# A hybrid attention trunk on one core: the last stage merges in wide chunks through scratch memory, then projects tile by tile

## The chip, the cores and the metric

The kernel runs on 1 core of one Trainium2 chip. The metric is device time in microseconds of one execution. The kernel before was timed in 3 runs: median 3657.09 us, 3652.93 to 3662.06.

## The reference, cut to what matters

One layer of an encoder for two groups of tokens: a prompt of 16 meta tokens and 2048 tokens, and 8 sample streams of 16 tokens. The kernel keeps them as 17 tiles of 128 tokens (0 to 15 of the prompt, and `s`).

```
(g_q, g_k, g_v, g_low, g_r, d_q, d_k, d_v, i_q, i_k, i_w, d_z, m_a, m_b) = split(h @ w_in)
o_a = gla_recurrence(...)                      # branch A, gated linear attention
y_a = (rmsnorm(o_a) * silu(g_r)) @ w_gla
o_b = attend(...)                              # branch B, attention over the 256 best keys
y_b = (o_b * silu(d_z)) @ w_dsa
merged = sigmoid(m_a + gate_b[0]) * y_a + sigmoid(m_b + gate_b[1]) * y_b
h_new  = layer_norm(ALPHA * h + merged @ w_out, ln_g, ln_b)
```

The last three products, with `w_gla`, `w_dsa` and `w_out` (1024 x 1024 each), are the stage that is changed. Every operand of a product is split into a high part (`h`, rounded to the format that TensorE takes) and the rest (`l`); a product is three matmuls, high by high, high by low and low by high.

## The kernel before, in words

Phase 1 makes the projections of `w_in` and writes them to scratch tensors in device memory (names `d_...`). Phase 2 runs the attention of branch B by blocks of 128 queries, from block 15 down to 8, with the recurrence of branch A beside it. The change begins where that ends (about 2690 us): the blocks of `LAST` (7, 6, 5, 0, 4, 2, 1, 3) are attended, and between them the generator `gla_project` is advanced, by the number that stands beside each block.

`gla_project` (L1355) makes `y_a`, gated: for each chunk of tokens (`PASSA` of them) it loads and splits the chunk's `d_oa` into the four pairs `xh`, `xl` (`x3`, L1333), and for each of 8 slices of 128 output channels it runs a group of 24 matmuls into the PSUM tile `pd` (`proj3`, L1349), multiplies by the row of gates `rma` (from `d_ma`) on VectorE and writes the result to `d_ya`. The slice's weights, 128 x 128, stand still in TensorE; the chunk's tokens are the moving columns, so a chunk's width is the matmul's width.

`finish` (L1385) then does the last stage in chunks of 256 tokens (one of 128). `merge` (L1373) is one chunk: 8 groups of 24 matmuls with `w_dsa`, and behind each group a multiply by `rmb` and an add of `rya` (VectorE), a rounding to `mgh` (ScalarE) and the rest `mgl` (GpSimd); `mgh` and `mgl` stay in SBUF, in two sets (`pm0`, `pm1`). The projection of a chunk takes, for each tile of 128 tokens, 48 matmuls of 512 columns into `fo` (L1413), and then the layer norm on VectorE and the store. Merges run two chunks ahead of it, so TensorE always has both kinds of matmul to choose from. `w3` (L1316) loads a weight matrix in 16 pieces, each through a raw buffer, a cast on ScalarE and a subtraction on VectorE or GpSimd.

The order on each engine is not the order of the code: a scheduler lays all instructions out by the code's order as priority and by when it reckons each is ready. Every engine then runs its list in order. All DMAs of this part are issued by one engine, SP, in order too; a load into a buffer waits there until the buffer is free, and what stands behind it waits along. Tile pools on the left and on the right of SBUF are stacks: a pool that is opened where another was closed waits for the last use of what lay there.

Of the kernel before, what the change touches and what calls it, by code (L numbers as in the profile page):

```python
# [10 lines left out]
F32 = mybir.dt.float32  # L11
F32R = mybir.dt.float32r
# [5 lines left out]
OP = mybir.AluOpType  # L18
PSUM = bass.MemoryType.PSUM
DRAM = bass.MemoryType.DRAM  # L20

P = 128
DM = 1024
KT = 8
META = 16
# [11 lines left out]
ALPHA = 2.0 ** 0.25  # L37
# [5 lines left out]
TURNS = "DAA", "DDA"  # L43
KLOW = 1040
HALF = 8
LAST = [(7, 0), (6, 2), (5, 1), (0, 1), (4, 2), (2, 1), (1, 1), (3, 0)]
NP3 = 256
EARLY = 1500
SKB = 3
POOL = "pkqx"  # L50
# [1 line left out]
PDB = 1  # L52
# [6 lines left out]
FKB = 3  # L59
WOM = 512  # L60
WOD = 1
KLAG = 1
FPACE = -5
PASSA = 9
SHORT = 8
NEARLY = 13
IDX_SCALE = (8 ** -0.5) * (64 ** -0.5)
TOPK = 256
# [6 lines left out]
ORDER = [t for p in PIECES for t in p if t != "m"]  # L75
NT = len(ORDER)
TT = META + NT * P
COL = {t: META + i * P for i, t in enumerate(ORDER)}
# [7 lines left out]
def nkeys(j):  # L86
    return META + P * (j + 1)
# [31 lines left out]
class Trunk:  # L119
# [73 lines left out]
    def scratch(self, ctx):  # L193
        dr = ctx.enter_context(self.tc.tile_pool(name="dr", bufs=1, space=DRAM))
        d = {}
        for n, s, t in (
            ("gq", [512, TT], F32), ("gk", [512, TT], F32), ("gl", [16, TT], F32), ("lf", [512, TT], F32),
            ("gv", [TT, 1024], F32), ("gr", [TT, 1024], F32),
            ("q", [2048, TT], F32R),
            ("ih", [512, TT], F32R), ("il", [512, TT], F32R),  # L200
            ("kd", [P, 4, TT], F32R), ("v", [TT, 256], F32), ("z", [TT, 1024], F32),
            ("ma", [1024, TT], F32), ("mb", [1024, TT], F32),
            ("oa", [1024, TT], F32), ("ob", [1024, TT], F32), ("ya", [1024, TT], F32), ("h", [TT, 1024], F32),
        ):
            d[n] = dr.tile(s, t, name="d_" + n)
        d["mask"] = {j: dr.tile([P, nkeys(j)], BF16, name=f"d_mask{j}") for j in range(16)}
        d["mask"]["s"] = dr.tile([P, SKEY], BF16, name="d_masks")
        d["xt"] = [dr.tile([P, KT, n], F32, name=f"d_xt{q}") for q, n in enumerate(PCN)]
        self.d = d
# [1027 lines left out]
    def phase2(self):  # L1237
        nc, tc, d = self.nc, self.tc, self.d
        with ExitStack() as main:
            early = ExitStack()  # L1240
            left = lambda n, bufs=1, **kw: early.enter_context(tc.tile_pool(name=n, bufs=bufs, **kw))
# [7 lines left out]
            right = lambda n, bufs=1, **kw: main.enter_context(tc.tile_pool(name=n, bufs=bufs, side="right", **kw))  # L1249
# [44 lines left out]
            inner.close()  # L1294
            tail = ExitStack()
            left = lambda n, bufs=1, **kw: tail.enter_context(tc.tile_pool(name=n, bufs=bufs, **kw))
            self.pm, self.pd = [left("pm0")], left("pd", PDB, space=PSUM)
            if PDB == 1:
                self.px.append(left("px2", space=PSUM))
            self.pw2, self.px3, self.pr, self.pe, self.pw = left("pw2"), left("px3"), left("pr", PRB), left("pe", 2), left("pw")  # L1300
            self.pm.append(left("pm1"))
            steps, self.turns = self.gla_project(), TURNS[1]
            next(steps)
            for j, n in LAST:
                for _ in self.attend(j):
                    pass
                for _ in range(n):
                    next(steps, None)
            self.flush()
            fin = self.finish()  # L1310
            next(fin)
        next(fin, None)
        tail.close()


    def w3(self, pool, src, name, width, most=512, raws=None, last=None):  # L1316
# [16 lines left out]
    def x3(self, name, c0, n):  # L1333

        xh = [self.px3.tile([P, 2, NP3], F32R, name=f"xh{k}") for k in range(4)]
        xl = [self.px3.tile([P, 2, NP3], F32R, name=f"xl{k}") for k in range(4)]
        for k in range(4):
            raw = self.pr.tile([P, 2, NP3], F32, name="raw")
            self.nc.sync.dma_start(raw[:, :, :n], self.d[name][2 * k * P : (2 * k + 2) * P, c0 : c0 + n].rearrange("(k p) t -> p k t", p=P))
# [3 lines left out]
    def rows3(self, name, c0, n, q):  # L1343

        t = self.pe.tile([P, NP3], F32, name="r" + name, tag="rb" if name == "mb" else "ra")
        self.nc.sync.dma_start(t[:, :n], self.d[name][q * P : (q + 1) * P, c0 : c0 + n])
# [8 lines left out]
    def gla_project(self):  # L1355

        ws = self.w3(self.pw, self.i["w_gla"][0], "w", P, last=self.pw2)
        w = -(-(TT - META) // (2 * PASSA)) * 2

# [10 lines left out]
                self.nc.sync.dma_start(self.d["ya"][q * P : (q + 1) * P, c0 : c0 + n], g)  # L1370
            yield

    def merge(self, wd, x, c0, n, pool):  # L1373

        mh = pool.tile([P, KT, NP3], F32R, name="mgh")
        ml = pool.tile([P, KT, NP3], F32R, name="mgl")
        for q in range(8):
            ya = self.rows3("ya", c0, n, q)
            t = self.rows3("mb", c0, n, q)
            self.tt(t, self.proj3(wd[q], x, n), t, OP.mult)  # L1380
            self.tt(t, t, ya, OP.add)
            self.split_sb(mh[:, q, :n], ml[:, q, :n], t)
        return mh, ml

    def finish(self):  # L1385

        nc, tc, i, d = self.nc, self.tc, self.i, self.d
        chunks = [(COL[j], 2 * P) for j in (15, 13, 11, 9, 7, 5, 1, 3)]
        chunks.insert(SHORT, (COL[0], P))
        x = self.x3("ob", *chunks[0])  # L1390
        wd = list(self.w3(self.pw, i["w_dsa"][0], "w", P, last=self.pw2))
        ready = [self.merge(wd, x, *chunks[0], self.pm[0])]
        ready.append(self.merge(wd, self.x3("ob", *chunks[1]), *chunks[1], self.pm[1]))
        yield
        with ExitStack() as c:
            pool = lambda n, bufs=1, **kw: c.enter_context(tc.tile_pool(name=n, bufs=bufs, **kw))
            cp, wk, pp = pool("fc"), pool("fk", FKB), pool("fo", 4, space=PSUM)
            self.pd = pool("pd2", 2, space=PSUM)
            wo = None
            for q, (c0, n) in enumerate(chunks):  # L1400
                if wo is None:
                    wo = list(self.w3(cp, i["w_out"][0], "wo", 512, WOM, wk))
                    lg = self.bcast_load(cp, i["ln_g"][0], DM, "lg3")
                    lb = self.bcast_load(cp, i["ln_b"][0], DM, "lb3")
                mh, ml = ready.pop(0)
                for s in range(0, n, P):
                    t = ORDER[(c0 + s - META) // P]
                    h = wk.tile([P, DM], F32, name="h3")
                    nc.sync.dma_start(h[:], d["h"][c0 + s : c0 + s + P, :])
                    for u in range(2):  # L1410
                        ps = pp.tile([P, 512], F32, name="fo")
                        wh, wl = wo[u]
                        self.mm3(ps[:], lambda k: mh[:, k, s : s + P], lambda k: ml[:, k, s : s + P],  # L1413
                                 lambda k: wh[:, k, :], lambda k: wl[:, k, :], KT)
                        cs = slice(512 * u, 512 * u + 512)
                        self.stt(h[:, cs], h[:, cs], ALPHA, ps[:], OP.mult, OP.add)
                    mu, rstd = self.ln_stats(wk, h[:], DM, P)
                    out = self.o["y_sample"].rearrange("b t d -> (b t) d") if t == "s" else self.o["y_prompt"][0, t * P : (t + 1) * P, :]
                    self.stt(h[:], h[:], mu, lg[:], OP.subtract, OP.mult)
                    cut = 2 if q == len(chunks) - 1 and s + P == n else 1  # L1420
                    for u in range(cut):
                        cs = slice(DM // cut * u, DM // cut * (u + 1))
                        self.stt(h[:, cs], h[:, cs], rstd, lb[:, cs], OP.mult, OP.add)
                        nc.sync.dma_start(out[:, cs], h[:, cs])
                if q + 2 < len(chunks):
                    nx = chunks[q + 2]
                    ready.append(self.merge(wd, self.x3("ob", *nx), *nx, self.pm[q % 2]))

    def setup(self, ctx):
        self.scratch(ctx)  # L1430
# [40 lines left out]
```

## Time and profile before

| | |
|---|---|
| median of 3 runs | 3657.09 us |
| profiled execution | 3653.39 us, its span 3651.6 us |
| busy in the span | PE 3516.6 us (96%), DVE 2568.0 (70%), ACT 1451.5 (40%), POOL 1048.6 (29%) |
| chain of waits, share of the span | PE 75%, DVE 13%, DMA 5% |
| mean granted clock of TensorE | 0.985 of full speed |

PE is TensorE's matmuls, PEld its weight loads, DVE VectorE, ACT ScalarE, POOL GpSimd, SP the engine that issues DMAs. Matmuls are pipelined: a matmul's time in a row is longer than the distance from its start to the next one's, so the cost of a run of matmuls is read from the starts. The same holds, less so, for DVE.

### The profile page before, as it was taken

How to read it: one execution, taken by the hardware profiler on the slowest of the kernel's cores; microseconds unless marked ns; L12 is line 12 of the kernel's file. 1: busy time of each engine (PE TensorE's matmuls, PEld its weight loads, DVE VectorE, ACT ScalarE, POOL GpSimd, SP SyncE). 2: the span in 40 equal slices, each digit the busy share in tenths (PEclk: the TensorE clock that was granted, in tenths of full speed). 3: DMA queues.
4: the chain of work that ended last, by engine and by line, in shares of the span. 5: the costliest groups of instructions: out<-in, count | busy, mean ns of one | idle time of the engine just before them, and what ended most of it. 6: DMA issues, size and time to landing. Idle time of an engine off the chain costs nothing.

```text
span 3651.6 us, 65899 instructions
## 1 busy us (share of the span) xinstructions
PE 3516.6 (96%) x24196; PEld 3224.6 (88%) x24196; DVE 2568.0 (70%) x5971; ACT 1451.5 (40%) x3084; POOL 1048.6 (29%) x1220
## 2 busy tenths in 40 slices
PE   7999999999999999999989999999999999989999
PEld 7999999999999999998976778777778888879998
DVE  7748997799999988943246877777765666555444
ACT  4444223433334234325434555555665443431110
POOL 3122343242343344344301433334410000012221
PEclk9999999999999999999999999999999999999999
DMA  8642443263442345363653333233343345564432
GB/s 266 196 127 84 136 124 96 84 180 106 122 127 75 117 136 166 115 173 122 160 170 106 84 92 85 80 92 85 85 116 89 94 106 138 150 193 140 121 114 62
DMA packets 535810, 448.78 MB, mean 123 GB/s; under 512 B 94032, under 2 KB 507856, under 8 KB 535488
## 3 DMA queue, kind: packets, MB, share of 16 engines
q1 hardware_dynamic: 535488, 444.58, 42.4%
q8 instruction: 190, 3.11, 0.4%
q14 instruction: 132, 1.08, 0.1%
HBM read 288.01 MB, written 156.44 MB: 122 GB/s over the span
## 4 chain that ended last, share of the span: by engine, by line
PE 75%; DVE 13%; DMA 5%; ACT 2%; issue 2%; POOL 1%; SPq 1%; POOLq 0%; DVEq 0%; ACTq 0%
PE pp L266 12%; PE pp L264 12%; PE pp L265 12%; PE oo L1070 6%; PE px L1046 4%; PE pd L264 3%; PE pd L266 3%; PE pd L265 3%; PE pl L1110 2%; PE pl L1111 2%; PE fo L264 2%; PE fo L265 2%; PE fo L266 2%; DVE junk L149 1%; DVE sc L152 1%
## 5 line engine op out<-in xcount | busy, mean ns | idle before, releaser
L149 DVE TENSOR_SCALAR_CACHE_REDUCE junk<-sc,cand 128x272 bf16<-128x272 f32 (+6 forms) x512 | 701.7, 1371 | 17.0
L143 POOL TENSOR_TENSOR wlo<-raw,whi 128x512 fp32r<-128x512 f32 x360 | 487.9, 1376 | 768.0 <-ACT whi L158 704.3
L266 PE MATMUL pp<-whi,xl 128*128 128x256 f32 (+3 forms) x1952 | 560.4, 288 | 4.4 <-DVE xl L143 4.4
L264 PE MATMUL pp<-whi,xh 128*128 128x256 f32 (+3 forms) x1952 | 561.7, 288 | 3.1 <-ACT whi L158 2.1
L264 PE MATMUL pp<-xh,whi 128*128 128x384 f32 (+2 forms) x1728 | 563.0, 326 | 1.4 <-ACT whi L158 1.4
L265 PE MATMUL pp<-xl,whi 128*128 128x384 f32 (+2 forms) x1728 | 563.2, 326 | 0.0
L266 PE MATMUL pp<-xh,wlo 128*128 128x384 f32 (+2 forms) x1728 | 562.1, 326 | 0.1
L265 PE MATMUL pp<-wlo,xh 128*128 128x256 f32 (+3 forms) x1952 | 560.9, 288 | 0.0
L266 PEld LDWEIGHTS pp<-whi,xl 128*128 128x128 f32 (+1 forms) x1952 | 370.4, 190 | 14.6 <-DVE xl L143 6.9
L264 PEld LDWEIGHTS pp<-whi,xh 128*128 128x128 f32 (+1 forms) x1952 | 371.4, 190 | 11.2 <-issue 3.0
L265 PEld LDWEIGHTS pp<-wlo,xh 128*128 128x128 f32 (+1 forms) x1952 | 371.4, 190 | 5.4 <-issue 2.3
L1112 DVE CUSTOM_DVE_ANT_0 lgl<-pl,mkl 128x348 f32<-128x348 f32 (+8 forms) x608 | 297.3, 510 | 83.6 <-PE pl L1111 48.0
L1110 PE MATMUL pl<-kd,q 128*128 128x348 f32 (+14 forms) x800 | 308.1, 388 | 32.7 <-DVE mx L1112 23.9
L264 PE MATMUL pd<-xh,wh 128*128 128x242 f32 (+3 forms) x1152 | 327.9, 285 | 8.6 <-ACT wh L1328 3.8
L264 PEld LDWEIGHTS pp<-xh,whi 128*128 128x128 f32 x1728 | 324.4, 188 | 2.7 <-ACT whi L158 2.0
L266 PE MATMUL pd<-xh,wl 128*128 128x242 f32 (+3 forms) x1152 | 324.6, 282 | 0.8 <-POOL wl L143 0.8
L265 PE MATMUL pd<-xl,wh 128*128 128x242 f32 (+3 forms) x1152 | 325.1, 282 | 0.3 <-DVE xl L143 0.3
L266 PEld LDWEIGHTS pp<-xh,wlo 128*128 128x128 f32 x1728 | 324.1, 188 | 1.2 <-POOL wlo L143 0.4
L265 PEld LDWEIGHTS pp<-xl,whi 128*128 128x128 f32 x1728 | 324.4, 188 | 0.7
L158 ACT CAST whi<-raw 128x512 fp32r<-128x512 f32 (+1 forms) x344 | 199.1, 622 | 314.8 <-DMA raw<-in_w_in 201.3
L155 ACT ACTIVATE lgl<-lgl,mx 128x1040 f32<-128x1040 f32 (+7 forms) x256 | 249.8, 976 | 181.5 <-DVE mx L1114 177.6
L1118 POOL COPY pmeta<-lgl 128x48 f32<-128x48 f32 x256 | 58.7, 229 | 771.4 <-ACT lgl L155 765.0
(250 smaller groups left out, 7842.7 us busy)
## 6 DMA issues: line engine op xcount, KB each, us to landing
raw<-in_w_in SPq DMA_DIRECT2D x360, 256.0 KB, 3.2
q<-d_q SPq DMA_DIRECT2D x272, 128.0 KB, 3.0
d_h<-x SPq DMA_DIRECT2D x17, 512.0 KB, 3.4
d_gv<-en SPq DMA_DIRECT2D x68, 128.0 KB, 2.1
d_gr<-en SPq DMA_DIRECT2D x68, 128.0 KB, 1.8
d_z<-en SPq DMA_DIRECT2D x68, 128.0 KB, 1.7
gr<-d_gr SPq DMA_DIRECT2D x17, 512.0 KB, 3.6
v<-d_gv SPq DMA_DIRECT2D x17, 512.0 KB, 3.9
```

The costliest lines, as they stand in the source:

```text
L143: (eng or self.nc.vector).tensor_tensor(out, a, b, op=op)
L149: (eng or self.nc.vector).tensor_scalar(out, a, s1, s2, op0=op0, op1=op1, **kw)
L155: self.nc.scalar.activation(out, a, f, **kw)
L158: (self.nc.vector.tensor_copy if self.spare else self.nc.scalar.copy)(out, src)
L264: mm(ps, ah(k), bh(k), start=k == 0, stop=False)
L265: mm(ps, ah(k), bl(k), start=False, stop=False)
L266: mm(ps, al(k), bh(k), start=False, stop=k == n - 1)
L1046: nc.tensor.transpose(ps[:, 2 * s + u, :], pe[u][a // KLOW][:, a % KLOW : a % KLOW + P], self.ident[:])
L1070: self.nc.tensor.matmul(oo[0][64 * o : 64 * o + 64, k : k + 2, :], self.v[:, s0 + s, d : d + 64], t[:, 2 * s : 2 * s + 2], start=self.fres ...
L1110: nc.tensor.matmul(ps[:, :m], q[:, u, :], kd, start=True, stop=False)
L1111: nc.tensor.matmul(ps[:, :m], q[:, 2 + u, :], kd, start=False, stop=True)
L1112: nc.vector.tensor_tensor_reduce(lg[z1][:, a : a + m], ps[:, :m], mk[z1][:, a : a + m], 1.0, NEG, OP.add, OP.max, mx[:, s : s + 1])
```

## The change

The merges no longer alternate with the projection. `MERGES` lists five chunks: tiles 13, 14, 15 and `s` (512 tokens), 9 to 12 (512), 6 to 8, 0 to 2 and 3 to 5 (384 each). The high and low parts of a merged chunk go to two new scratch tensors, `d_mh` and `d_ml`; the rounding is written over the buffer of `rya`, the rest over that of `rmb`, and both are written from there. The first chunk is emitted ahead of block 1 in `LAST`, inside the attention; the other four come after it, when `w_out` is being loaded. Then 17 tiles are projected: each tile's `mh` and `ml` (512 KB each) are read back, into one set of buffers (`m0`, which is there early) or three more (`m1`, which lie where the merges' pools lay). `gla_project` runs in 5 chunks (436 tokens, one of 432) for 9 (242, one of 240).

```diff
-LAST = [(7, 0), (6, 2), (5, 1), (0, 1), (4, 2), (2, 1), (1, 1), (3, 0)]
-NP3 = 256
+LAST = [(7, 0), (6, 1), (5, 1), (0, 0), (4, 1), (2, 1), (1, 0), (3, 0)]
+NP3 = 512
-PASSA = 9
-SHORT = 8
+PASSA = 5
+MTB = 3
+MERGES = [(13, 4), (9, 4), (6, 3), (0, 3), (3, 3)]
...
             for j, n in LAST:
+                if j == 1:
+                    next(merges)
                 for _ in self.attend(j):
...
+        self.finish(merges, tail)
...
+    def merges(self):
+        x, wd = None, None
+        for t, n in MERGES:
+            c0, n = COL[t], n * P
+            x = self.x3("ob", c0, n)
+            wd = wd or list(self.w3(self.pw, self.i["w_dsa"][0], "w", P, last=self.pw2))
+            for q in range(8):
+                ya = self.rows3("ya", c0, n, q)
+                t = self.rows3("mb", c0, n, q)
+                self.tt(t, self.proj3(wd[q], x, n), t, OP.mult)
+                self.tt(t, t, ya, OP.add)
+                hi, lo = ya.bitcast(F32R), t.bitcast(F32R)
+                self.split_sb(hi, lo, t)
+                for name, z in ("mh", hi), ("ml", lo):
+                    self.move(self.d[name][q * P : (q + 1) * P, c0 : c0 + n], z)
+            yield
...
+            for _ in merges:
+                pass
+            before.close()
+            m1 = c.enter_context(self.tc.tile_pool(name="fm1", bufs=MTB))
+            for q, t in enumerate(tiles):
+                mp = m1 if q % (MTB + 1) else m0
+                m = [mp.tile([P, KT, P], F32R, name="m" + x) for x in "hl"]
+                for z, name in zip(m, ("mh", "ml")):
+                    self.move(z[:], d[name][:, COL[t] : COL[t] + P].rearrange("(k p) t -> p k t", p=P))
```

What stands on the engines is shown at three places (line numbers of the kernel after are up to 4 higher).

TensorE where the last attention block (3) ends and the next stage begins. `oo` are the products with the values, `pl` and `px` transposes and logits, `pd` the groups of 24. Before:

```order
L266 MATMUL pd<-xh_36807,wl_31690 128x240
L1070 MATMUL oo<-pt,v 64x256
L1070 MATMUL oo<-st_37446,v 64x256
L1070 MATMUL oo<-pt,v 64x256
L1070 MATMUL oo<-st_37446,v 64x256
L1070 MATMUL oo<-pt,v 64x256
L1070 MATMUL oo<-st_37439,v 64x256
L1070 MATMUL oo<-pt,v 64x256
L1070 MATMUL oo<-st_37439,v 64x256
L989 MATMUL pl<-ident,pt 128x128 x4
L1082 MATMUL oo<-pm,vm 128x512
L264 MATMUL pd<-xh_37523,wh_37547 128x256
```

The same place now:

```order
L1112 MATMUL pl<-kd_21205,q 128x264
L1113 MATMUL pl<-kd_21205,q 128x264
L1048 MATMUL px<-ident,lgl 128x128 x8
L1080 MATMUL px<-ident,pmeta 96x128 x3
L1048 MATMUL px<-ident,lgl 128x128 x6
L1080 MATMUL px<-ident,pmeta 96x128
L1072 MATMUL oo<-pt,v 64x256
```

Before, groups of `gla_project` stand between the attention's matmuls to the very end of block 3. Now the last such group (of the first merge) stands 150 matmuls ahead of the end, and all between are the attention's.

TensorE where the merges end and the projection goes on, now (before, `pd` and `fo` rows alternate to the end and there is no such place):

```order
L266 MATMUL pd<-xh_37894,wh_35825 128x384
L267 MATMUL pd<-xl_37898,wh_35825 128x384
L268 MATMUL pd<-xh_37894,wl_35826 128x384
L266 MATMUL fo<-woh_36907,mh 128x512
L267 MATMUL fo<-wol_36908,mh 128x512
```

and the DMAs that SP issues there (`mh_38273` and `ml_38274` belong to the tile that TensorE takes next):

```order
L172 DMA d_mh_75<-rya_38125 128x384
L172 DMA d_ml_76<-rmb_38127 128x384
L172 DMA mh_38273<-d_mh_75 128x8x128
L172 DMA ml_38274<-d_ml_76 128x8x128
L172 DMA mh_38341<-d_mh_75 128x8x128
L172 DMA ml_38342<-d_ml_76 128x8x128
L172 DMA d_mh_75<-rya_38160 128x384
L172 DMA mh_38409<-d_mh_75 128x8x128
```

One tile (48 matmuls of `fo`) is spread among the merges before this place, and 768 rows of `fo` follow it without a `pd` between them; the first load of `mh` here waits for the last `pd` matmul.

SP where `w_dsa` begins to load, now (before, these loads stand at the end of block 3; now at the beginning of block 1's attention):

```order
L1340 DMA raw_35747<-d_ob_72 128x2x512
L1033 DMA z_36177<-d_z_68 128x512
L1340 DMA raw_35751<-d_ob_72 128x2x512
L1371 DMA d_ya_73<-rma_35702 128x432
L172 DMA q_36240<-d_q_63 64x4x128
L1328 DMA raw_35757<-in_w_dsa 128x4x128
```

The first piece of `w_dsa` goes through the same two raw buffers as the chunk's `d_ob`, behind its third and fourth piece, and TensorE has 28 attention matmuls between its last `gla_project` matmul and the first one that needs that piece.

## Rows read from the trace of the kernel before

**Rows 1.** The page: PE's busy tenths in 40 slices of the span.

```profile
PE   7999999999999999999989999999999999989999
```

**Rows 2.** Windows: stretch, length, busy us of each engine, PEclk, DMA share, GB/s.

```profile
3231.00:3240.00 9.00, 2.59 (x17) 1.51 (x13) 3.27 (x5) 2.72 (x5) 0.00 (x0) 0.87 0.58 174
3240.00:3250.00 10.00, 7.83 (x41) 6.75 (x40) 3.64 (x7) 3.96 (x8) 2.53 (x3) 0.78 0.89 272
3250.00:3260.00 10.00, 8.57 (x41) 7.90 (x42) 6.89 (x11) 6.13 (x11) 3.19 (x3) 0.66 0.80 251
...
3230.00:3300.00 70.00, 58.22 (x340) 50.73 (x339) 35.34 (x58) 26.80 (x48) 17.94 (x16) 0.90 0.72 223
...
3295.00:3620.00 325.00, 324.20 (x2153) 298.74 (x2152) 149.19 (x271) 40.85 (x93) 68.27 (x78) 1.00 0.38 114
```

**Rows 3.** Timeline of PE: start us, us, matmul; first and last of unbroken runs.

```profile
1846.87 0.34 PE L265 MATMUL pp<-xl,whi 128*128 128x384 f32 x1
...
1848.95 0.33 PE L265 MATMUL pp<-xl,whi 128*128 128x384 f32 x1
...
3219.99 0.27 PE L264 MATMUL pd<-xh,wh 128*128 128x240 f32 x1
...
3222.57 0.27 PE L266 MATMUL pd<-xh,wl 128*128 128x240 f32 x1
...
3262.03 0.28 PE L264 MATMUL pd<-xh,wh 128*128 128x256 f32 x1
...
3263.58 0.28 PE L265 MATMUL pd<-xl,wh 128*128 128x256 f32 x1
...
3589.04 0.27 PE L266 MATMUL pd<-xh,wl 128*128 128x128 f32 x1
...
3593.17 0.28 PE L264 MATMUL pd<-xh,wh 128*128 128x128 f32 x1
...
3641.22 0.39 PE L265 MATMUL fo<-wol,mgh 128*128 128x512 f32 x1
...
3642.80 0.39 PE L266 MATMUL fo<-woh,mgl 128*128 128x512 f32 x1
```

**Rows 4.** Timeline of PE at the old boundary; in brackets idle before, and its releaser.

```profile
3236.73 0.49 PE L1082 MATMUL oo<-pm,vm 96*128 96x512 f32 x1 [4.12 <-DVE pm L143]
3239.52 0.58 PE L264 MATMUL pd<-xh,wh 128*128 128x256 f32 x1 [2.29 <-ACT wh L1328]
```

**Rows 5.** DMA issues from 2690 us: count, KB each, median us to landing.

```profile
h<-d_h SPq DMA_DIRECT2D x17, 512.0 KB, 4.0
rmb<-d_mb SPq DMA_DIRECT2D x64, 128.0 KB, 2.3
...
d_ya<-rma SPq DMA_DIRECT2D x64, 121.0 KB, 2.6
...
raw<-in_w_dsa SPq DMA_DIRECT2D x16, 256.0 KB, 3.5
```

**Rows 6.** Groups by form, 3240 to 3651 us: busy us, mean ns, idle before.

```profile
L143 POOL TENSOR_TENSOR mgl<-rmb,mgh 128x256 fp32r<-128x256 f32 x64 | 51.3, 802 | 152.5 <-ACT mgh L158 152.5
L143 DVE TENSOR_TENSOR rmb<-rmb,rya 128x256 f32<-128x256 f32 x64 | 27.4, 429 | 1.8
L158 ACT CAST mgh<-rmb 128x256 fp32r<-128x256 f32 x64 | 26.0, 406 | 214.7 <-DVE rmb L143 214.6
L143 DVE TENSOR_TENSOR xl<-raw,xh 128x512 fp32r<-128x512 f32 x28 | 20.9, 745 | 30.1 <-ACT xh L158 29.5
L158 ACT CAST xh<-raw 128x512 fp32r<-128x512 f32 x28 | 17.4, 620 | 28.4 <-PE pd L266 13.8 <-DMA raw<-d_ob 11.5 <-PE fo L265 3.0
```

**Rows 7.** Timeline of DVE in block 3's attention.

```profile
3199.49 0.43 DVE L1112 CUSTOM_DVE_ANT_0 lgl<-pl,mkl 128x264 f32<-128x264 f32 x1
...
3199.84 0.43 DVE L1112 CUSTOM_DVE_ANT_0 lgl<-pl,mkl 128x264 f32<-128x264 f32 x1
...
3200.26 1.28 DVE L1056 COPY pt<-px 128x512 f32<-128x512 f32 x2
3201.46 0.68 DVE L143 TENSOR_TENSOR pt<-z,rs 128x512 f32<-128x512 f32 x1
```

More of the change, by code (lines that the diff above doesn't have):

```diff
@@ L203, in scratch @@
             ("oa", [1024, TT], F32), ("ob", [1024, TT], F32), ("ya", [1024, TT], F32), ("h", [TT, 1024], F32),
+            ("mh", [1024, TT], F32R), ("ml", [1024, TT], F32R),
         ):
@@ L1296, in phase2 @@
             left = lambda n, bufs=1, **kw: tail.enter_context(tc.tile_pool(name=n, bufs=bufs, **kw))
-            self.pm, self.pd = [left("pm0")], left("pd", PDB, space=PSUM)
+            self.pd = left("pd", PDB, space=PSUM)
             if PDB == 1:
@@ L1300, in phase2 @@
             self.pw2, self.px3, self.pr, self.pe, self.pw = left("pw2"), left("px3"), left("pr", PRB), left("pe", 2), left("pw")
-            self.pm.append(left("pm1"))
             steps, self.turns = self.gla_project(), TURNS[1]
             next(steps)
+            merges = self.merges()
             for j, n in LAST:
+                if j == 1:
+                    next(merges)
                 for _ in self.attend(j):
@@ L1309, in phase2 @@
             self.flush()
[L1310 to L1313, printed above, removed]
+        self.finish(merges, tail)
     def w3(self, pool, src, name, width, most=512, raws=None, last=None):
@@ L1371, in gla_project @@
             yield
[L1373 to L1394, printed above, removed]
+    def merges(self):
[14 more added lines that the diff above has]
+            yield
@@ L1395, in finish @@
+    def finish(self, merges, before):
+        nc, i, d = self.nc, self.i, self.d
         with ExitStack() as c:
-            pool = lambda n, bufs=1, **kw: c.enter_context(tc.tile_pool(name=n, bufs=bufs, **kw))
-            cp, wk, pp = pool("fc"), pool("fk", FKB), pool("fo", 4, space=PSUM)
+            pool = lambda n, bufs=1, **kw: c.enter_context(self.tc.tile_pool(name=n, bufs=bufs, side="right", **kw))
+            cp, wk, m0, pp = pool("fc"), pool("fk", FKB), pool("fm0"), pool("fo", 4, space=PSUM)
@@ L1398, in finish @@
             self.pd = pool("pd2", 2, space=PSUM)
[L1399 to L1427, printed above, removed]
@@ new lines, in finish @@
+            wo = list(self.w3(cp, i["w_out"][0], "wo", 512, WOM, wk))
+            lg = self.bcast_load(cp, i["ln_g"][0], DM, "lg3")
+            lb = self.bcast_load(cp, i["ln_b"][0], DM, "lb3")
+            for _ in merges:
+                pass
+            before.close()
+            m1 = c.enter_context(self.tc.tile_pool(name="fm1", bufs=MTB))
+            tiles = [ORDER[ORDER.index(t) + k] for t, n in MERGES for k in range(n)]
+            for q, t in enumerate(tiles):
[3 more added lines that the diff above has]
+                    self.move(z[:], d[name][:, COL[t] : COL[t] + P].rearrange("(k p) t -> p k t", p=P))
+                h = wk.tile([P, DM], F32, name="h3")
+                nc.sync.dma_start(h[:], d["h"][COL[t] : COL[t] + P, :])
+                for u in range(2):
+                    ps = pp.tile([P, 512], F32, name="fo")
+                    self.mm3(ps[:], lambda k: m[0][:, k, :], lambda k: m[1][:, k, :],
+                             lambda k: wo[u][0][:, k, :], lambda k: wo[u][1][:, k, :], KT)
+                    cs = slice(512 * u, 512 * u + 512)
+                    self.stt(h[:, cs], h[:, cs], ALPHA, ps[:], OP.mult, OP.add)
+                mu, rstd = self.ln_stats(wk, h[:], DM, P)
+                out = self.o["y_sample"].rearrange("b t d -> (b t) d") if t == "s" else self.o["y_prompt"][0, t * P : (t + 1) * P, :]
+                self.stt(h[:], h[:], mu, lg[:], OP.subtract, OP.mult)
+                cut = 2 if t == tiles[-1] else 1
+                for u in range(cut):
+                    cs = slice(DM // cut * u, DM // cut * (u + 1))
+                    self.stt(h[:, cs], h[:, cs], rstd, lb[:, cs], OP.mult, OP.add)
+                    nc.sync.dma_start(out[:, cs], h[:, cs])
```

## The prediction

> **What bounds the kernel now.** I read the page's slices first, then the windows of the stretch that changes, then TensorE's timeline in it. TensorE is busy in nine tenths or more of nearly every slice [rows 1], and between 3295 and 3620 us it is busy for 324.2 of 325 us at full clock [rows 2]: there time is the number of matmuls times the distance between their starts, and nothing else. The one hole is the boundary between the last attention block and the last stage. From 3230 to 3300 us TensorE is busy for 58.2 of 70 us, so 11.8 us are idle; and in the windows from 3240 and from 3250 us its granted clock is 0.78 and 0.66, a mixture of its two levels (1.2 and 2.4 GHz) that followed idle time of 4.12 and 2.29 us [rows 2, 4]. Against full clock that loses 2.2 and 3.4 us. The boundary costs 11.8 + 5.6 = 17.4 us.
>
> **Wider matmuls: a sure gain.** Distances between starts, from first and last of unbroken runs [rows 3]: 128 columns (3593.17 - 3589.04) / 37 = 0.112 us; 240 columns 2.58 / 23 = 0.112; 256 columns 1.55 / 13 = 0.119; 384 columns 2.08 / 12 = 0.173; 512 columns 1.58 / 7 = 0.226. So there is a floor of 0.112 us below about 240 columns, and above it 256 more columns cost 0.107 us; 432 and 436 columns I put between 384 and 512, at 0.193 and 0.195.
>
> Gated projection: before, 9 chunks x 8 groups x 24 = 1728 matmuls x 0.112 = 193.9 us. Now 768 x 0.195 + 192 x 0.193 = 186.6 us. Gain 7.3 us.
> Merges: before, 1536 x 0.119 + 192 x 0.112 = 204.5 us. Now 384 x 0.226 + 576 x 0.173 = 186.5 us. Gain 18.0 us.
> The projection keeps its 17 x 48 matmuls of 512 columns. Together 25.3 us less for an engine that bounds this part. The distances are measured, so the ends are narrow: 23 to 27.
>
> The Trainium skill ("TensorE: Matmul & The Clock Gate", section "Wait — 56ns, not 53.3ns?") says that matmuls start N / 2.4 GHz + about 2.5 ns apart: 55.6 ns for 128 columns, 215.7 for 512. By that rule the 1536 matmuls that go would bring 1536 x 2.5 ns = 3.8 us and not 25.3, as the columns stay the same. The rows for 128 and 240 columns disagree with it (0.112 us for both); they are what I go by. It is the fourth rival below.
>
> **The boundary moves.** `w_dsa` and the first merge now start inside block 1's attention, so the end of the attention meets ready weights, and the wait for `wh` (2.29 us) and those behind it go. What stays is the attention's own end: 4.12 us until `pm` [rows 4]. And the first group of the second merge writes PSUM that the attention gives back only after the last `ob`, one VectorE instruction (0.6 to 0.7 us, like the last row of [rows 7]) and a handover later: 1.1 us. With 2 us for the clock (half of 4 us, the smaller of the two windows) that is 7.2 us for 17.4: gain 10.2 us, between 8 and 12.
>
> **What it adds: five gaps on TensorE.**
>
> 1. Start of `w_dsa`. Its first piece comes behind the chunk's `d_ob` in two raw buffers. From the moment the last `gla_project` group has used its first pair of `xh`: cast of a 128x1024 pair 1.1 us and subtraction 1.4 (twice 620 and 745 ns less a start-up) [rows 6], then the third piece of `d_ob`, 512 KB, 4.0 us [rows 5], cast and subtraction 2.5, then the piece of `w_dsa` 3.5 us [rows 5], cast 0.6: about 13.2 us. TensorE has 18 matmuls x 0.193 left of its group and some 30 short attention matmuls: 7.3 us. It waits 5.9 us, and 2 us go to the clock: 7.9. Ends 3 and 11: the 2.29 us of [rows 4], where the same load was late; and all of the 4.0 us load added again.
>
> 2. Block 3's attention without cover. Its last 150 matmuls now stand alone: 46 logit matmuls of 264 columns, 70 transposes, 32 value products of 256 columns of which two run side by side. By [rows 3] that is 46 x 0.122 + 70 x 0.112 + 32 x 0.119 = 17.3 us of TensorE. VectorE has 23 logit passes, starting 0.35 us apart, 9 copies 0.60 apart [rows 7], six more of 0.6 to 0.7 for the two halves' ends, two subtractions of 1.4 for the next chunk, a merge's multiply and add 1.3, and 14 short ones: 23 us. Before, all that ran beside `pd` groups. Now the slower engine sets the pace: at least 5.7 us of TensorE idle, and more as each step of the softmax waits for the one before. I take 9; ends 4 (VectorE runs partly ahead) and 18 (TensorE at half clock needs 35 us for its 17).
>
> 3. The merge's two row buffers. A group's buffers now come free only when both parts have been written to memory. Cycle of one buffer at 384 columns: multiply, add, cast at 1.5 times [rows 6] 0.64 + 0.64 + 0.61, GpSimd 1.2 (a scaled-up 802 ns, so an upper value), the write 2.6, the reload 2.3 [rows 5], handovers 0.4: 8.4 us. Two groups of TensorE take 48 x 0.173 = 8.3 us: no reserve, and SP issues four DMAs for each group, in order, each waiting in it; behind it the next group's writes queue. The two PSUM buffers let TensorE run one group ahead, and the 48 matmuls of the first tile (10.8 us) fill in between. While `w_out` loads (16 pieces through three buffers, between the merge's own DMAs on SP and ScalarE) the second merge is as tight. I take 3 us, between 0 and 20.
>
> 4. Changes of chunk inside the merges: four pieces of `d_ob` through two raw buffers again. Two of the changes have the first tile's matmuls beside them, the last has none: 1.5 us, between 0 and 4.
>
> 5. Merges to projection. The first `mh` after the merges goes to where the last weights of `w_dsa` lie, and waits for the last `pd` matmul. Then 0.4 us of issue and 512 KB, 4.0 us [rows 5], with `ml` 0.5 us behind it: 5 us idle, 2 us of clock: 7, between 5 and 9. Behind that load on SP stand the next tiles' loads, which only that tile's successors wait for.
>
> At nothing I count the tiles that follow: a tile is 48 x 0.226 = 10.8 us of TensorE, and its 2 MB of traffic (`mh`, `ml`, `h`, result) makes 190 GB/s, where [rows 2] shows 272 in one window; four sets of buffers give each load 30 us. If that cover goes, each us late in 16 tiles costs 16 us. The end of the kernel (layer norm of the last tile) is as it was.
>
> Sum: -25.3 - 10.2 + 7.9 + 9 + 3 + 1.5 + 7 = -7.1 us. From the profiled execution's 3653.4 us this makes 3646; the median of the runs shown is 3.7 us above that execution, so for a median I say **3650 us**.
>
> **Rivals.**
>
> A. The gaps are smaller than I make them, since the scheduler's list leaves TensorE some attention to do: gap 1 costs 3, gap 2 only the difference of the two engines at 4.5, gap 3 nothing, gap 4 1, gap 5 without clock 5. Sum 13.5 for 28.4, so 22 us less than before: 3635. For it speaks that TensorE was busy through all attention blocks before [rows 1]; against it, that the list puts nothing between the rows of block 3's end.
>
> B. The other side: the write and reload of the merges becomes the bound. With all DMAs on one queue and writes landing like the 512 KB loads do (4.0 us for 2.6), the cycle is 9.8 to 10.1 us for 8.3 of TensorE. That costs 0.8 to 0.9 us for each of 24 groups, about 20 us, less the filling tile where it helps, and some 5 us in the second merge: 16 more than the sum, 3666. It decides from a cycle of about 8.9 us on, where the gain of 7 is used up. For it: the reserve is nil. Against it: the old rows of 128 KB landed in 2.3 us while the stretch moved 114 GB/s [rows 2, 5], and two PSUM buffers.
>
> C. Block 3 falls to the lower clock for all of its bare stretch: gap 2 costs 18, sum +2, 3659: no change that can be measured. For it, the drop to 0.66 and 0.78 after idle time of 2 to 4 us [rows 2, 4].
>
> D. The rule on distances holds and the wide matmuls bring 3.8 us: sum +14.4, 3671. The measured 0.112 us at 128 columns speaks against it.
>
> **How the numbers follow.** 0.3% is about what a measurement of this kernel can tell from no change, 11 us: 3646 to 3668. My forecast (3642 to 3657) has 0.45, A 0.28, B 0.15, C 0.09, D 0.03. Faster by over 0.3%: all of A and a sixth of the forecast, 0.35. Slower: D, C's upper part, and B where it costs more than 18 us: 0.18. The same: the rest, 0.47. The forecast's own range is 3642 to 3657; with A below and most of B above it, and for the ends of gaps 2 and 3, 3628 to 3674 should hold the time 8 times in 10.
>
> **What would show it.** Right: starts of `pd` 0.173 and 0.226 us apart; a gap of 4 to 8 us ahead of the first merge with a wait for `wh`; VectorE as the releaser of most idle time in block 3's last 25 us; 4 to 6 us idle before the second tile's `fo`, released by a DMA; the projection after it without gaps. Wrong: `pd` waiting for `rmb` again and again in the three merges of 384 (B), or waits for `mh` in the projection, which I count at nothing; and a bare block 3 that takes under 20 us (A).

## The result, and the profile after

The kernel after takes 3683.41 us (median of 4 runs, 3681.19 to 3684.54), the kernel before 3657.32 beside it: ratio 1.007, interval 1.0053 to 1.0088. It is 26 us slower; forecast were 3650 and a range of 3628 to 3674. The profiled execution took 3682.5 us, its span is 3680.6.

The page's slices of TensorE, beside [rows 1], have two nines fewer in the last quarter, and nothing that stands out:

```profile
PE   7999999999999999999989999999998999989899
```

First, windows. This one of before covers the stretch in which the new stage's first generator starts (columns as in [rows 2]):

```profile
2690.00:2830.00 140.00, 130.48 (x961) 105.06 (x957) 79.58 (x292) 80.57 (x173) 15.98 (x34) 0.96 0.41 111
```

And these are of the kernel after: the same stretch, the start of `w_dsa`, block 3's bare end, the merges, the change to the projection, the projection.

```profile
2691.00:2831.00 140.00, 126.30 (x858) 95.72 (x858) 83.29 (x316) 81.88 (x175) 14.87 (x36) 0.95 0.35 94
3200.00:3240.00 40.00, 35.01 (x170) 26.83 (x169) 22.56 (x58) 19.31 (x43) 13.74 (x18) 0.91 0.73 212
3283.00:3318.00 35.00, 25.42 (x138) 17.09 (x137) 17.98 (x60) 13.25 (x29) 2.64 (x10) 0.80 0.50 137
3318.00:3487.00 169.00, 160.66 (x816) 147.09 (x816) 67.33 (x99) 35.63 (x59) 36.07 (x32) 0.98 0.71 223
3487.00:3507.00 20.00, 14.50 (x51) 11.53 (x52) 2.81 (x5) 0.51 (x1) 1.72 (x2) 0.83 0.78 208
3510.00:3660.00 150.00, 150.00 (x654) 122.56 (x653) 75.55 (x107) 0.00 (x0) 19.27 (x14) 1.00 0.57 175
```

Five of these places the prediction had named. The first it had not: 858 matmuls for 961 in a stretch of 140 us, long before anything that it priced. The next rows say why. TensorE's first matmul of the gated projection, before and after:

```profile
2737.69 0.36 PE L264 MATMUL pd<-xh,wh 128*128 128x242 f32 x1
```

```profile
2827.60 0.45 PE L266 MATMUL pd<-xh,wh 128*128 128x436 f32 x1
```

It comes 90 us later. ScalarE's timeline shows the first cast of a `w_gla` piece before (2704.48, as soon as its load lands) and after (behind the last `lgu` of block 8 and its transposes):

```profile
2704.48 0.62 ACT L1328 CAST wh<-raw 128x512 fp32r<-128x512 f32 x1 [2.02 <-DMA raw<-in_w_gla]
```

```profile
2790.17 0.39 ACT L156 ACTIVATE lgu<-lgu,mx 128x128 f32<-128x128 f32 x1
...
2793.73 1.14 ACT L1329 CAST wh<-raw 128x512 fp32r<-128x512 f32 x2
```

The piece itself was loaded in time (SP issued it at 2702.95). The cast waits for space. `px3` grew from 16 to 32 KB a partition, `pr` and `pe` by 4 KB each, and `pm0` (16 KB) went: the pool `pw` with the first six weight slices lies 8 KB higher. Before, it ended 384 bytes below the buffers of `lgu` (the logits of the upper keys, blocks 15 to 8); now it reaches 7.6 KB into them. The pool waits as a whole: `wh0`, which doesn't touch `lgu`, waits too. (`px3` also begins 16 KB lower now, over other buffers of the upper blocks; e1 below leaves it where it was.) Without `pd` groups between them the attention's matmuls wait for VectorE and ScalarE.

To see what each place costs I take the mean distance from one start to the next at full clock without idle time, over both traces, for each kind of matmul (attention 0.129 us; `pd` 0.120 at 242 and 256 columns, 0.178 at 384, 0.205 at 436, 0.232 at 512; `fo` 0.2295), and call lost what a stretch lasts beyond the sum of its matmuls. Some records are missing, so a column's sum stands to about 6 us.

| lost us, by stretch | before | after | e1 | e2 | e7 | e6 | e9 |
|---|---|---|---|---|---|---|---|
| to 2831 | 19 | 29 | 29 | 16 | 32 | 16 | 16 |
| 2831 to 3200 | 3 | 8 | 12 | 9 | 10 | 9 | 8 |
| 3200 to the attention's end | 2 | 31 | -2 | 24 | 19 | 7 | 7 |
| from there to the last `pd` | 13 | 12 | 17 | 14 | 14 | 8 | 9 |
| change to the projection | - | 9 | - | 9 | 8 | 8 | 0 |
| the rest | 9 | 9 | 9 | 9 | 9 | 9 | 9 |
| sum | 46 | 98 | 64 | 80 | 92 | 57 | 48 |

(e1 to e9 are experiments, below.) After loses 52 us more than before and its matmuls cost 24 less: 28, the difference of the spans being 29. (Each entry is rounded for itself, so a column can miss its sum by one.)

What TensorE waited for from 2691 us on, after (us in total, times, longest):

```profile
PE px L1048 <- ACT lgl L156: 8.4, 10, 2.3
PE pd L266 <- DVE rmb L144: 6.0, 5, 2.6
PE fo L266 <- DMA mh<-d_mh: 5.8, 1, 5.8
PE pl L1112 <- DVE mx L1114: 5.5, 12, 1.2
PE pl L1112 <- DMA q<-d_q: 5.0, 5, 2.2
```

The attention's own waits are the largest together: it stands bare at both ends. The second and third lines are gaps 3 and 5 of the prediction.

### The profile page after: what moved, and what is told of

Read it like the earlier page. It is cut to its first block, busy times and chain, and to the rows that moved or that the text cites. A ratio compares the mean times of both kernels' runs of the same rounds, so it can differ in the third digit from the quotient of the medians.

```text
span 3680.6 us, 62470 instructions
## 1 busy us (share of the span) xinstructions
PE 3514.4 (95%) x22660; PEld 3176.2 (86%) x22660; DVE 2558.8 (70%) x5843; ACT 1439.8 (39%) x3020; POOL 1046.5 (28%) x1188
## 4 chain that ended last, share of the span: by engine, by line
PE 65%; DVE 17%; DMA 7%; issue 5%; ACT 3%; POOL 2%; SPq 1%; POOLq 0%; DVEq 0%; ACTq 0%
PE pp L268 10%; PE pp L266 10%; PE pp L267 10%; PE oo L1072 6%; PE px L1048 4%; DVE junk L150 4%; PE pl L1112 2%; PE pl L1113 2%; DVE lgl L1114 2%; PE pd L266 2%; PE pd L267 2%; PE pd L268 2%; PE fo L268 2%; PE fo L267 2%; PE fo L266 2%
## 5 line engine op out<-in xcount | busy, mean ns | idle before, releaser
L1112 PE MATMUL pl<-kd,q 128*128 128x348 f32 (+14 forms) x800 | 311.6, 392 | 42.2 <-DVE mx L1114 29.5
L1072 PE MATMUL oo<-pt,v 128*64 128x256 f32 x1088 | 264.6, 392 | 7.3 <-DVE pt L1058 5.7
L1048 PE MATMUL px<-ident,lgl 128*128 128x128 f32 x1600 | 252.4, 280 | 17.4 <-ACT lgl L156 8.6
L1113 PE MATMUL pl<-kd,q 128*128 128x348 f32 (+14 forms) x800 | 265.6, 335 | 0.0
```

Source lines behind the costliest of these rows:

```text
L1048: nc.tensor.transpose(ps[:, 2 * s + u, :], pe[u][a // KLOW][:, a % KLOW : a % KLOW + P], self.ident[:])
L1072: self.nc.tensor.matmul(oo[0][64 * o : 64 * o + 64, k : k + 2, :], self.v[:, s0 + s, d : d + 64], t[:, 2 * s : 2 * s + 2], start=self.fres ...
L1112: nc.tensor.matmul(ps[:, :m], q[:, u, :], kd, start=True, stop=False)
L1113: nc.tensor.matmul(ps[:, :m], q[:, 2 + u, :], kd, start=False, stop=True)
```

## The experiments

Theory 1: the late start of the gated projection costs time by itself. Theory 2: the attention has too little covering work at its end, and TensorE idles at the lower clock there. Rival to both: the merges' write and reload chain (rival B of the prediction). Ratios are to the kernel before, run beside each; intervals in brackets. The kernel before took 3657 to 3658 us beside e1 to e10, 3651 beside e12 and e13, and 3653 beside e14 and e15, so between these groups only ratios compare.

**e1: the late start alone, in the kernel before.** Two pools in the other order, so that the weights lie on `lgu` there too.

```diff
-            ..., left("pe", 2), left("pw")
-            self.pm.append(left("pm1"))
+            ..., left("pe", 2), None
+            self.pm.append(left("pm1"))
+            self.pw = left("pw")
```

> The kernel before with two pools opened in the other order: the weights' pool (six of the eight slices of w_gla) now lies above pm1, on the last attention blocks' logit buffers (lgu), as in the kernel after. Nothing else is changed. Theory 1 (the late start of the gated projection costs time by itself): the first pd moves from 2738 us to about 2820 us as in the kernel after, the stretch to 2830 us loses some 10 us more, and the time is 3664 to 3672. Rival (its matmuls are only done later, beside other attention, so the late start is free): 3653 to 3661.

3679.61 us, ratio 1.0062 [1.0049, 1.0076]: 22 us slower, for no operation added or taken away, and with `px3` where it lay before. Its first `pd` and its window, beside the ones of before and after above:

```profile
2830.87 0.28 PE L264 MATMUL pd<-xh,wh 128*128 128x242 f32 x1
```

```profile
2691.00:2831.00 140.00, 126.42 (x861) 95.19 (x860) 84.13 (x322) 83.58 (x180) 15.45 (x38) 0.95 0.32 85
```

The late start is shown to cost time by itself; I had priced it at half. By the table 10 us go in this stretch and 9 more up to 3200 us; behind that e1 loses as much as before (15 us to the last `pd` in both). What makes up the 9 I haven't traced.

**e2: the early start alone, in the kernel after.** Only what the first groups need lies on free space: three slices, `px3`, `pr`, `pe`; the other slices lie where the keys and `lgu` were, and are loaded behind the first chunk.

```diff
-            self.pw2, ..., self.pw = left("pw2"), ..., left("pw")
+            self.pw2, ... = left("pw2"), left("px3"), left("pr", PRB), left("pe", 2)
+            self.pw, self.pw3 = left("pw"), left("pw3")
...
-        first = [next(ws) for _ in range(6)]
+        first = [next(ws) for _ in range(3)]
...
+            if name == "w":
+                pool = self.pw if a < 3 * P else self.pw3 if a == 3 * P else self.pw2
```

> The kernel after with the tail's pools laid out so that three weight slices, x, raw buffers and rows lie on space that is free at 2700 us (one slice on lgu's place, four on the keys'). Theory 1 as the cause of the whole: the gated projection starts near 2740 us again, the 10 to 17 us lost up to 3197 us come back, time 3666 to 3673. Theory 2 (the attention has only so much covering work; what is done early is missing at the end): the list's bare run of attention matmuls in block 3 grows from 150 to 236, each of which lost about 0.12 us in the kernel after, so 10 us go there: 3678 to 3690.

3670.05 us, 1.0036 [1.0023, 1.005]: 13 of the 26 us are back. The window to 2831 us, the stretch with block 3's now longer bare run (from 3249 us on), and its last 24 us:

```profile
2691.00:2831.00 140.00, 130.25 (x892) 104.04 (x890) 82.27 (x297) 80.20 (x178) 15.33 (x33) 1.00 0.40 110
3240.00:3304.00 64.00, 51.38 (x328) 37.91 (x326) 42.67 (x145) 30.08 (x71) 9.12 (x27) 0.92 0.59 171
3280.00:3304.00 24.00, 18.58 (x139) 13.73 (x137) 15.47 (x55) 10.96 (x26) 2.08 (x9) 1.00 0.45 123
```

The 236 bare matmuls (counted in the list, as the 150) lost about as much as the 150 had: by the table, the loss from 3200 us on is 24 us for 31. From 3280 to 3304 us they ran at full clock, where the kernel after stood at 0.80 in its own bare run. So bare attention doesn't have a fixed price for each matmul, as theory 2 had it.

**e3, e7, e6: merges inside block 3.** e3 emits the second merge ahead of block 3, e7 the third too, e6 is e7 with the layout of e2.

```diff
-                if j == 1:
+                if j in (1, 3):
                     next(merges)
```

```diff
-                if j == 1:
+                for _ in range({1: 1, 3: 2}.get(j, 0)):
                     next(merges)
```

> The kernel after with the second merge chunk emitted ahead of block 3 too, so that its groups stand between block 3's attention matmuls (the bare run falls from 150 to 5). Theory 2 (a lone attention block leaves TensorE idle and at the lower clock): of the 17.4 us lost between 3283 and 3318 us about 14 come back, time 3666 to 3672. Rival (the merges' write and reload chain bounds the merges wherever they stand): pd waits for rmb within block 3 and no more than 5 us come back, 3678 to 3684.

> The kernel after with the second and third merge chunks emitted ahead of block 3, but with the pools as they are in the kernel after, so that the gated projection starts late. Beside the run that has both edits (3643) and the one with the layout alone (3670) it parts the two. Theory (the late start costs by itself, whatever stands at the end, 13 to 22 us by the two runs that moved it alone): 3656 to 3665. Rival (only the merges' place counted, the early start gives its time back at the end): 3643 to 3650. If a third chunk early adds nothing to a second one: 3674 to 3679.

> The kernel after with the layout of the pools that lets the gated projection start early, and with the second and third merge chunks emitted ahead of block 3. Theories 1 and 2 together: early cover and late cover, 10 to 15 us of the start and 14 to 17 us of the end come back, 3652 to 3660. If only the end counts: 3666 to 3672. If the write and reload chain bounds the merges: 3675 or more.

e3: 3677.05 us, 1.0054 [1.004, 1.0069]. e7: 3673.56, 1.0044 [1.0028, 1.006]. e6: 3643.24, 0.9962 [0.9952, 0.9972], faster than the kernel before. Blocks 1 and 3 from 3280 to 3360 us, of e7 and then of e6:

```profile
3280.00:3360.00 80.00, 75.78 (x409) 61.16 (x408) 39.20 (x102) 25.43 (x49) 17.17 (x23) 0.98 0.71 216
```

```profile
3280.00:3360.00 80.00, 78.35 (x475) 68.53 (x473) 39.30 (x114) 25.25 (x53) 16.43 (x27) 1.00 0.65 198
```

Block 3's loss falls from 17 us to 5 in e7 and to none in e6. Yet e3 and e7 gained 6 and 10 only, and three of my expectations missed: e3's of 14; e7's, that the late start costs 13 to 22 us beside the early merges too (it costs 30); and e6's 3652 to 3660, 9 us too slow. Layout alone is worth 13 us, merges alone 10, both 40. The attention ends at 3358 us in e7 and at 3361 in e6, but by then e6 has 408 `pd` matmuls left to do and e7 552: 144 matmuls, some 26 us of TensorE, for the same attention. That is how I read the 40: the early start gives the lead, and it is kept only where the end has cover too.

**e5: the width of the gated projection alone.** The kernel after with nine chunks of 242.

```diff
-LAST = [(7, 0), (6, 1), (5, 1), (0, 0), (4, 1), (2, 1), (1, 0), (3, 0)]
+LAST = [(7, 0), (6, 2), (5, 1), (0, 1), (4, 2), (2, 2), (1, 0), (3, 0)]
...
-PASSA = 5
+PASSA = 9
```

> The kernel after with the gated projection in nine chunks of 242 tokens again (buffers unchanged, still a late start). Its groups end later in the list, so that the bare run of 150 matmuls in block 3 is gone. Theory (width brings some 9 us, 1728 x 0.1195 less 960 x 0.2048; the bare run costs 14): 3683 + 9 - 14, 3674 to 3682. Rival (width alone matters): 3690 to 3695. By the rule on distances (the width brings 2 us): 3668 to 3673.

3695.95 us, 1.0108 [1.0088, 1.0127]: 12.5 us slower than after. My theory missed: block 3 has groups of `pd` to its end, but the first merge now comes after the attention, and 36 us of idle time stand there instead, nearly all of it in these two waits:

```profile
3253.00:3497.00 244.00, 207.66 (x1008) 183.36 (x1008) 98.08 (x132) 56.35 (x90) 57.80 (x47) 0.95 0.73 228
```

```profile
PE pd L266 <- DVE rmb L144: 18.7, 10, 6.2
PE pd L266 <- ACT wh L1329: 14.5, 1, 14.5
```

The edit moves the groups too, so the time alone doesn't price the width. Reckoned as in the table, e5 loses 96 us and after 98: the idle time has only changed its place, and some 10 us are left for the width. The Trainium skill's rule ("TensorE: Matmul & The Clock Gate", section "Wait — 56ns, not 53.3ns?"), by which I estimate 1.9 us for 768 matmuls fewer, is measured there on matmuls back to back. It doesn't agree with these figures, from a stream in which each matmul has a weight load of its own ([rows 2]: 2152 for 2153).

**e9: the change to the projection.** e6, and the last merge chunk takes first the four slices that lie where the tiles' buffers will be.

```diff
-            for q in range(8):
+            for q in (4, 5, 6, 7, 0, 1, 2, 3) if c == len(MERGES) - 1 else range(8):
```

> The kernel with both edits (pools laid out for the early start, second and third merge ahead of block 3), and the last merge chunk takes the four slices first whose weights lie where the tiles' buffers will be, so these come free four groups before the last pd. Theory (the gap between the merges and the projection is the wait for the pool, 5 us idle and 3 us of clock): that wait goes, 6 to 8 us less than 3643: 3635 to 3638. Rival (the loads of the tiles, 1 MB each, then compete with the merges' rows): 3640 to 3645.

3637.26 us, 0.9943 [0.9922, 0.9963]. The 20 us after the last `pd`, in e6 and in e9:

```profile
3453.00:3473.00 20.00, 14.84 (x54) 11.63 (x53) 3.13 (x5) 0.51 (x1) 1.76 (x2) 0.83 0.79 210
```

```profile
3457.00:3477.00 20.00, 20.00 (x89) 16.42 (x89) 11.13 (x17) 1.03 (x2) 5.08 (x4) 1.00 0.71 208
```

The gap was the pool's wait: it is gone, and some 6 us of time with it, as forecast (the ratios' intervals overlap).

**e10, e13, e12, e14, e15: the row buffers.** e10 is e9 with three row buffers of each kind and `ln_g`, `ln_b` loaded later. e13 and e12 are e9 with `ln_g`, `ln_b` later and `rmb` in a pool above the weights, two buffers of each row in e13, three in e12. e14 is the kernel after, e15 is e9, with three for `rmb` alone.

```diff
-        t = self.pe.tile([P, NP3], ...)
+        t = (self.pb if name == "mb" else self.pe).tile([P, NP3], ...)
```

> The kernel of the run before (early start, merges early, tiles' buffers early) with three row buffers of each kind for two in the merges; ln_g and ln_b are loaded later, to make room. Theory (two row buffers cost the merges what is idle before pd for rmb, 2 to 8 us in the traces): 3 to 6 us less than the run before. Rival (those waits come from the DMAs on SP's queue, not from the number of buffers): no change within 2 us.

> The control of the next run: early start, merges early, tiles' buffers early, ln_g and ln_b loaded later, and the merges' rows rmb in a pool of their own (two buffers) on lgu's place, above the weights, so that all that the first groups of the gated projection need lies on free space. If the miss of the run with three row buffers (3657) came from its weights' being pushed 3.7 KB into lgu's place and starting late: first pd near 2725 us again and 3634 to 3640. If it came from the late load of ln_g and ln_b: 3650 or more.

> The same with three buffers of each row in the merges. Theory (two row buffers cost the merges the idle time before pd for rmb, some 4 us of the 8.9 lost between the attention's end and the last pd): 2 to 5 us less than the control. Rival (the rows come late because of SP's queue and the changes of chunk, not for want of a buffer): within 1.5 us of it.

> The kernel after with three buffers for the row rmb in the merges and two for rya as before; nothing else is changed, and the order of the matmuls up to block 3's end stays. It prices the two row buffers in the kernel after itself. Theory (they cost what is idle before pd for rmb, 6.0 us, and part of it only, since rya still has two): 2 to 5 us less than 3683, 3678 to 3682. The price by the pair of runs before (13 us): 3668 to 3673. None: 3682 to 3685.

> The run with the early start, the early merges and the early tiles' buffers (3637 beside 3657 of the kernel before, 0.9943), with three buffers for rmb and with ln_g and ln_b where they were. If three buffers alone bring what the run with three of each row showed: a ratio of 0.991 to 0.993 to the kernel before (some 3625 to 3632). If the third rya is what counts: 0.994.

e10: 3656.96 us, 1.0 [0.9989, 1.0011], 20 us slower than e9. One reason I had overlooked: 4 KB more of rows push the first slices into `lgu` once more, and its first `pd` starts at

```profile
2809.50 0.36 PE L266 MATMUL pd<-xh,wh 128*128 128x436 f32 x1
```

Unplanned, it is one more showing of the late start, but says nothing of the buffers. Nor is the start all of the 20 us. e13, which starts early again (2719 us), takes 3640.89, 0.997 [0.9957, 0.9983]: by the ratios 11 us less than e10, but 10 more than e9, so it lies between its two forecasts. Whether these 10 come from the late load of `ln_g` and `ln_b` or, in e13, from the place of `rmb`, no run has parted; its waits for `rmb` are 9.7 us, e9's 4.1. e12: 3627.76, 0.9928 [0.9912, 0.9943]. The waits of e13 and then of e12:

```profile
PE pd L266 <- DVE rmb L144: 9.7, 8, 2.5
...
PE fo L266 <- DMA mh<-d_mh: 2.5, 1, 2.5
```

```profile
PE pd L266 <- DVE rmb L144: 4.4, 4, 2.3
```

Third buffers of both rows bring 13 us against e13, where 2 to 5 were forecast, and 5 against e9 by the ratios, whose intervals overlap. e14: 3679.31, 1.0066 [1.0052, 1.008], and e15: 3633.58, 0.9943 [0.9931, 0.9956]: a third `rmb` alone brings 1.5 us to the kernel after and nothing to e9 by the ratios (4 us each by the medians), not more than the intervals allow for no change. So in the kernel after itself the two `rmb` buffers cost little; its two `rya` buffers no run has priced. Whether the third `rya` (the gated projection uses its buffers too) makes up the rest of e12's gain, alone or with the late `ln_g`, wasn't tried apart. e12 is the fastest version by its ratio: 0.72% under the kernel before, 1.4% under the kernel after.

## Why the prediction was wrong, point by point

**The step that failed is one that it doesn't have: the start of the gated projection.** Its parts began with the matmuls' widths and the old boundary; the generator's start, where wider buffers move every pool behind them, stood at nothing without being named. "Against it" and "at nothing" were weighed for 3100 us and later; the loss began at 2704. In after it costs 10 us to 2831 and 5 more to 3200; put alone into the kernel before 22, taken alone out of after 13, and taken out where the merges stand early 30. The order of the instructions told it ahead of any run: from 2690 us on, TensorE's trace has some 275 matmuls of the attention before the first `pd` in the kernel before, and some 840 in the kernel after, and TensorE runs its list in order. The second step is a size: the merges lost 7 us more than gaps 3 and 4 had.

**Wider matmuls, -25.3.** Right in sum: at full clock the 1728 `pd` of the gated projection cost some 206 us before, the 960 now 196; the merges' cost 206 and 191. That is 24, though the halves differ: some 10 for the gated projection where 7.3 were forecast, 15 for the merges' 18.0. e5 bears out the first half. The way there differs too. These are unbroken runs, as in [rows 3], at 436 columns:

```profile
2907.25 0.36 PE L266 MATMUL pd<-xh,wh 128*128 128x436 f32 x1
...
2909.84 0.36 PE L267 MATMUL pd<-xl,wh 128*128 128x436 f32 x1
```

2.59 / 13 = 0.199 us for 0.195 forecast, so the distances alone would have brought 193.9 - 191 = 3 us; the rest I put down to handovers, of which 40 groups have fewer with the attention than 72; no run parts that.

**The boundary, 7.2 left, and gap 2, 9.** Together 16.2 forecast, 17.5 measured for 3280 to 3317. That the sizes agree is partly luck, for the make-up is another. 9.6 of the 35 us from 3283 are idle; the rest, some 8 us, went to half clock (0.80 at the mean), which is rival C's mechanism, though not for all of the stretch. And VectorE wasn't the releaser of most idle time, as I had said: of 9.5 us of waits from 3280 to 3317 it ended 3.8, ScalarE 3.3 and one load of `q` 2.2. The pairs of value products show the clock, at 3292 us and 20 us later:

```profile
3292.17 0.63 PE L1072 MATMUL oo<-pt,v 128*64 128x256 f32 x1
...
3292.60 0.63 PE L1072 MATMUL oo<-pt,v 128*64 128x256 f32 x1
...
3312.87 0.38 PE L1072 MATMUL oo<-pt,v 128*64 128x256 f32 x1
...
3313.08 0.38 PE L1072 MATMUL oo<-pt,v 128*64 128x256 f32 x1
```

0.43 us from pair to pair, and 0.21: the lower of the two levels after idle times of 1.4 and 0.8 us, and the full one later in the same bare run. Blocks 1 and 3 ahead of it, with the first merge beside them, lost 5 us that I had not counted.

**Gap 1, 7.9.** Right in size, by luck: 9.0 from 3200 to 3240, at a clock of 0.91. It was no single wait for `wh`, as I had said, but short ones of the attention that stood there, the longest 1.4 us.

**Gaps 3 and 4, 4.5.** 11.5 measured, 7 too few. The DMAs behind them, beside [rows 5]:

```profile
rmb<-d_mb SPq DMA_DIRECT2D x24, 192.0 KB, 2.6
d_mh<-rya SPq DMA_DIRECT2D x24, 192.0 KB, 2.3
...
raw<-d_ob SPq DMA_DIRECT2D x10, 384.0 KB, 4.6
```

The cycle's parts came as estimated, so rival B in its form (writes of 4 us) didn't happen; TensorE waits for `rmb` 5.1 us in this stretch, and e14 finds no gain clear of noise from a third `rmb`. The rest, among it 1.8 us before a `pd` for `xh` at a change of chunk, no run has parted. Where all merges stand behind the attention, as in e5, the same wait grows to 18.7 us, so the chain of the rows isn't out of the question as a cost.

**Gap 5, 7.** Right, 8.7:

```profile
3486.36 0.34 PE L268 MATMUL pd<-xh,wl 128*128 128x384 f32 x1
3492.50 0.76 PE L266 MATMUL fo<-woh,mh 128*128 128x512 f32 x1 [5.80 <-DMA mh<-d_mh]
```

**The tiles, nothing.** Right: 150.00 of 150 us busy at full clock, though the stretch moves 175 GB/s; a matmul of `fo` takes 0.230 us at the mean for 0.228 to 0.229 before, 1 to 2 us in all.

Added up, against the forecast: the late start 10 to 2831 us, 5 to 3200, 5 in blocks 1 and 3, 7 in the merges, 5 for the widths, the change, gap 1 and the bare end, 1 to 2 for `fo`: some 33 of the 36 us between the sum (3646) and the profiled execution (3682.5). The rule on distances (rival D, 3671) came nearer to the time for another reason; the 24 us that the widths brought speak against it, where it has 3.8.

## What to carry to other kernels

When a buffer grows, look first at what every pool behind it now lies on, and compare where the first instruction of each changed stage stands in its engine's list: 384 bytes of reserve were worth 22 us here. Work that covers another stage's waits counts where it stands, not only how much of it there is; to move the start of the cover or its end alone gave back 13 and 10 us of 40. Before a size is changed for speed, price the space that it takes as one of the terms.

## What the runs showed of the hardware

Two stretches of bare attention with alike shares of idle time (9.6 of 35 us from 3283 in after, 5.4 of 24 us from 3280 in e2) ran at a mean granted clock of 0.80 and of 1.00. Their single idle times differ. In after the clock was at 0.50 from 3287 to 3294 and from 3301 to 3307 us, and an idle time of 1.4 us stands ahead of the first, one of 2.2 us at the start of the second. In e2 it was at 0.50 from 3256 to 3266 us, earlier in its bare run, with an idle time of 3.5 us at the start; from 3280 on no single idle time is over 0.7 us. After, and then e2:

```profile
3284.90 0.33 PE L1048 MATMUL px<-ident,lgl 128*128 128x128 f32 x1 [1.42 <-ACT lgl L156]
...
3301.53 0.56 PE L1112 MATMUL pl<-kd,q 128*128 128x264 f32 x1 [2.24 <-DMA q<-d_q]
```

```profile
3256.43 0.60 PE L1112 MATMUL pl<-kd,q 128*128 128x272 f32 x1 [3.52 <-DVE mx L1114]
```

That is what these runs show; which bare stretch the clock will spare, none of them tests.
